# Gates, last weights and last-row operands of a Fourier-Hyena layer issued at other places, and one sum in another pool

## The chip, the cores and the metric

The kernel runs on one core of a Trainium2 chip. The metric is the device time of one execution in microseconds, the median of several. The engines are TensorE (PE in the profile; PEld is its weight load), VectorE (DVE), ScalarE (ACT), GpSimd (POOL) and SyncE (SP, which here only issues DMAs). Every engine runs its instructions in the order in which the program holds them.

## The reference

Two sequences of 1024 rows and 1024 channels go through one layer, each by itself. What is computed, cut to its steps:

```python
p = rmsnorm(x, g_pre) @ w_in
fv, fg, hv, hg, mg = jnp.split(p, [F_WIDTH, 2 * F_WIDTH, 2 * F_WIDTH + 3 * H_WIDTH,
                                   2 * F_WIDTH + 4 * H_WIDTH], axis=-1)
fz = jnp.fft.fftn(fv grouped by 256 channels, axes=(1, 3), norm="ortho").real
y_f = (fz * jax.nn.silu(fg)) @ w_fourier_out
v, x1, x2 = jnp.split(short_conv(hv, w_short), 3, axis=-1)
kf = hyena_filters(...)
z = v
for n, gate in enumerate((x1, x2)):
    z = gate * long_conv(z, kf[:, n], hyena_d[n])
y_h = (z * jax.nn.silu(hg)) @ w_hyena_out
g_f, g_h = jnp.split(jax.nn.sigmoid(mg + b_merge), 2, axis=-1)
out = (g_f * y_f + g_h * y_h) @ w_out
return x + rmsnorm(out, g_post)
```

The long convolution is one of length 2048 in the frequency domain.

## The kernel before, in words

A product of two f32 matrices is made of three matmuls. Each operand is split (`split`, L168) into a rounded part `h`, which ScalarE makes as a cast, and the rest `l`, a subtraction on VectorE or GpSimd; `hh`, `hl` and `lh` are summed (`mm3`). So every weight block of 128x512 comes as one DMA (`wr` or `mraw`), one cast (`wh`) and one subtraction (`wl`). `split` keeps the cast's instruction as `self.rounded`.

The stages, by the span's time: the Fourier branch (0 to 222 us); the Hyena filters (to 650); the branches (`branches`, to about 1700); the remaining gates of the second sequence (`phase_gates`, to 1942); the two output projections and the merge (`phase_out`, to 2302); the product with `w_out` and the last norm (`last_rows`, to the end).

`branches` runs 30 convolutions, steps (sequence b, order n, channel block c). A round of the loop issues `front` and `gates` of step i+1 and then `conv_back` of step i: its products with the filter (`k`, a DMA for each of eight groups), the spectrum `y`, its split into `yh` and `yl`, and the inverse transform `pT`. `gates` makes the multiplier `x` of a step. For b = 0 and n = 1 it also makes the SiLU gate: two halves `sg` of 128x512, loaded from memory for the early blocks (SyncE) or read from PSUM for the others, a Silu on ScalarE, and a multiply `x <- x, sg` on GpSimd. The slots of `sg` have the tag `gt`, three of them, which `gt` copies of other gates use too. GpSimd also makes the `wl` of the input projections (`pin`) here and stores `wh` and `wl` for later use.

`phase_gates` runs jobs of seven block products in place of eight (sums of blocks of both operands in advance). `kept` (L1052) copies a partial product out of PSUM: `u` into a slot of its own, `m` and `v` into the slots tagged `w` of pool `wp`, two of them, which the raw weights `wr` of `phase_out` take afterwards.

`phase_out` runs four units (a sequence and a half of it), each with 16 projections of 24 matmuls (`pyf` for Fourier, `pyh` for Hyena). Each projection takes two weights (`weight`: DMA issued by GpSimd, cast on ScalarE, subtraction on VectorE), and `gated` loads a gate `g`, opens it by a Sigmoid on ScalarE and multiplies. `ahead` splits the operands of the next pass. `beside` spreads the preparation of `w_out` over units 1 and 2: `load` in one step and `blocks` two steps later (split of blocks into `bh` and `bl`, sums, split of sums into `th` and `tl`, two stores to `d_t`). In unit 3 `sum4` loads a stored sum (`t4l`) and splits it into `t4h` and `t4l` at once.

`last_rows` runs eight jobs of seven products (`po`). `prepare` loads the merged rows (`mraw`, by GpSimd), splits blocks into `wh`, `wl` and sums of blocks (`ms`) into `mxh`, `mxl`. In a job's loop `kept` copies `u` and `v`; `prepare` of the next job is written behind the copy of `v`, and the products of T4 come last.

The order on each engine comes from a scheduler that works from the written program; `tc.issue_after(ins)` makes what is issued under it stand behind the instruction `ins` where both are on one engine. A tile that takes a slot of a pool waits until the slot's last user is done.

Of the kernel before, what the change touches and what calls it, by code (L numbers as in the profile page):

```python
# [16 lines left out]
P = 128  # L17
# [144 lines left out]
class K:  # L162
# [5 lines left out]
    def split(self, h, l, src, eng="pool", heng="act"):  # L168
        nc = self.nc
        if heng == "act":  # L170
            self.rounded = nc.scalar.copy(h, src)  # L171
        else:
            nc.vector.tensor_copy(h, src)
        self.sub(eng, l, src, h)

# [3 lines left out]
    def tt(self, eng, out, a, b, op):  # L179
        e = self.nc.gpsimd if eng == "pool" else self.nc.vector  # L180
        e.tensor_tensor(out, a, b, op=op)  # L181

# [3 lines left out]
    def sub(self, eng, out, a, b):  # L186
        self.tt(eng, out, a, b, SUB)

# [718 lines left out]
    def branches(self, nb, nct, ws):  # L907
# [10 lines left out]
        plain = list(self.PLAIN)  # L918
        Z, X = {}, {}

# [5 lines left out]
        def gates(i):  # L926
            b, n, c = steps[i]
            x = self.conv(2 + n, c, ws, f"x{n + 1}", b)
            if n and b == 0:
                early = c < NH  # L930
                ps = None if early else self.inproj(4, c)
                for q in range(2):
                    sg = self.wp.tile([P, 512], F32, tag="gt", name="sg", bufs=3)
                    if early:
                        nc.sync.dma_start(sg, self.d_g[0][4][c][:, 512 * q:512 * q + 512])
                    with tc.issue_after(self.turned.ins):
                        nc.scalar.activation(sg, sg if early else ps[:, 512 * q:512 * q + 512], AF.Silu)
                    self.mul("pool", x[:, 512 * q:512 * q + 512], x[:, 512 * q:512 * q + 512], sg)
            X[i] = x
        B = front(0)  # L940
        gates(0)
        for i, (b, n, c) in enumerate(steps):
            nxt = None
            if i + 1 < len(steps):
                nxt = front(i + 1)
                gates(i + 1)
                if i + 2 < len(steps) and steps[i + 2][0] != steps[i + 1][0]:
                    self.load_x(steps[i + 2][0])
            y = self.conv_back(n, c, B, ws)
            B = nxt  # L950
            for _ in range({4: 2, 3: 2, 2: 2, 1: 2}.get(len(steps) - i, 0)):
                self.spill_gate(b, *plain.pop(), ws)
            z = self.gate(n, c, y, X.pop(i))
            if n == 0:
                Z[c] = z
                continue
            nc.sync.dma_start(self.d_sh[b][c], z)
            if b == 0 and NF <= c:
                self.spill_gate(0, 0, c, ws)
# [22 lines left out]
    def phase_gates(self):  # L982
# [6 lines left out]
        with ExitStack() as es:  # L989
# [61 lines left out]

            def kept(p, own=False):  # L1052
                t = gw.tile([P, 512], F32, tag="u", name="u", bufs=1) if own else wp.tile([P, 512], F32, tag="w", name="m", bufs=2)
                copied = nc.scalar.copy(t, p)
                if own:
                    self.copied = copied
                return t
# [8 lines left out]
            for i, (sec, c) in enumerate(jobs):  # L1066
# [5 lines left out]
                self.times(pa, A["s1"], T1, False)  # L1072
                v = kept(pa)
                out(sec, c + 1, 1, pc, v, SUB)
# [16 lines left out]
    def phase_out(self):  # L1091
# [6 lines left out]
        with ExitStack() as es:  # L1098
# [17 lines left out]
            def weight(w, dt, q):  # L1116
# [9 lines left out]
                self.split(h.rearrange("p a b -> p (a b)"), l.rearrange("p a b -> p (a b)"), r, "dve", "act")  # L1126
                self.weighed = self.rounded
                return h, l
# [33 lines left out]
            def beside(i, dt):  # L1162

                with tc.issue_after(self.fetched.ins), tc.issue_after(self.opened.ins):
                    if i in (1, 2):
# [3 lines left out]
                        elif part == 3:  # L1169
                            blocks(k, self.raw)  # L1170
                    if (i, dt) == (3, 1):
# [14 lines left out]
            def blocks(k, r):  # L1186
# [5 lines left out]
                BL.append(l)  # L1192
                self.sums(s, r)
                h, l = [bl.tile([P, 2, 512], F32R, tag=f"{t}{k}", name=f"{t}{k}", bufs=1) for t in ("th", "tl")]
                self.split(h, l, s[:, 1:3], "dve", "act")
# [12 lines left out]
            def sum4(k):  # L1208
                h, l = [sp.tile([P, 512], F32R, tag=f"yf{2 * k + j}", name=f"t4{'hl'[j]}{k}", bufs=1) for j in range(2)]
                r = l.bitcast(F32)  # L1210
                nc.sync.dma_start(r, self.d_t[1][:, k])
                self.split(h, l, r, "dve", "act")
                T4.append((h, l))
# [31 lines left out]
    def last_rows(self, units, B11, B21, B22, T1, T2, T3, T4, gp, op):  # L1245
# [38 lines left out]
        def kept(p, own=False):  # L1284
            t = wp.tile([P, 512], F32, tag="gt" if own else "w", name="u" if own else "m", bufs=3 if own else 2)
            nc.scalar.copy(t, p)
            return t
# [10 lines left out]
        for i, (u, t) in enumerate(jobs):  # L1298
# [32 lines left out]
            self.times(pa, A["s2"], T2, False)  # L1331
            w = kept(pa, True)
            pc = self.psum("T", 2, "po")
            self.times(pc, A["s3"], T3, True)
            self.times(pa, A["s1"], T1, False)
            v = kept(pa)
            half_row(1, 1, pc, v, SUB, "pool")
            last = (A, pa, pc)
            if i + 1 < len(jobs):
                A = prepare(i + 1)  # L1340
                pa, pb, m1 = first(A)
            A_, pa_, pc_ = last

# [95 lines left out]
```

## Time and profile before

| | us |
|---|---|
| median of 3 runs (lowest to highest) | 2466.59 (2461.57 to 2469.35) |
| profiled execution | 2470.75 |
| its span, first to last instruction | 2469.0 |
| VectorE busy | 1912.8 |
| ScalarE busy | 1064.4 |
| GpSimd busy | 499.0 |
| mean granted TensorE clock | 0.994 of full |

A row of the timeline has the start, the duration, the engine, the line, the operation, what it writes and reads, and in brackets the idle time of the engine just before it with what ended that wait. The view of waits has a row for each kind of wait: its total, how often, and the longest. A row of DMA issues (SPq or POOLq, or POOL with DMA_DIRECT2D) gives the time of the issue, not of the transfer.

### The profile page before, as it was taken

How to read it: one execution, taken by the hardware profiler on the slowest of the kernel's cores; microseconds unless marked ns; L12 is line 12 of the kernel's file. 1: busy time of each engine (PE TensorE's matmuls, PEld its weight loads, DVE VectorE, ACT ScalarE, POOL GpSimd, SP SyncE). 2: the span in 40 equal slices, each digit the busy share in tenths (PEclk: the TensorE clock that was granted, in tenths of full speed). 3: DMA queues.
4: the chain of work that ended last, by engine and by line, in shares of the span. 5: the costliest groups of instructions: out<-in, count | busy, mean ns of one | idle time of the engine just before them, and what ended most of it. 6: DMA issues, size and time to landing. Idle time of an engine off the chain costs nothing.

```text
span 2469.0 us, 36969 instructions
## 1 busy us (share of the span) xinstructions
PE 2407.5 (98%) x13196; PEld 2086.9 (85%) x13196; DVE 1912.8 (77%) x3597; ACT 1064.4 (43%) x1919; POOL 499.0 (20%) x516
## 2 busy tenths in 40 slices
PE   6999999999999999999999999999999999999998
PEld 6988888888788888888888888888788788787786
DVE  7687898998649999899889999866556455665677
ACT  5546576766433333333222222323444344444343
POOL 1331213221342443331000000112100111112121
PEclk9999999999999999999999999999999999999999
DMA  7535655555555455545443443435444567775443
GB/s 274 183 122 205 217 182 166 169 180 168 171 174 179 159 176 163 172 149 203 137 134 131 143 142 131 133 128 176 161 162 158 193 218 255 237 268 194 156 160 128
DMA packets 225153, 429.37 MB, mean 174 GB/s; under 512 B 23542, under 2 KB 87255, under 8 KB 224456
## 3 DMA queue, kind: packets, MB, share of 16 engines
q1 hardware_dynamic: 198444, 333.34, 40.7%
q0 software_dynamic: 26336, 93.65, 10.7%
q8 instruction: 104, 1.70, 0.3%
q14 instruction: 81, 0.66, 0.1%
q10 hardware_dynamic: 188, 0.02, 0.0%
HBM read 290.60 MB, written 136.31 MB: 173 GB/s over the span
## 4 chain that ended last, share of the span: by engine, by line
PE 44%; DMA 4%; issue 4%; DVE 1%; POOL 1%; ACT 1%; SPq 0%; DVEq 0%; POOLq 0%; ACTq 0%
PE pin L194 17%; PE pg L194 8%; PE po L194 6%; PE pT L194 4%; PE pyf L194 4%; PE pX L194 4%; PE pyh L194 1%; DMA wr<-in_w_ho 1%; DMA wr<-in_w_fo 1%; POOL wr L1123 1%; PE tph L791 1%; DMA mraw<-d_m 1%; DMA d_m<-yf 1%; DMA t4l<-d_t 0%; DMA d_g<-gt 0%
## 5 line engine op out<-in xcount | busy, mean ns | idle before, releaser
L194 PE MATMUL pin<-xh,wl 128*128 128x512 f32 x1472 | 578.7, 393 | 3.3 <-POOL wl L181 3.3
L194 PE MATMUL pin<-xh,wh 128*128 128x512 f32 x1472 | 578.9, 393 | 1.1 <-DMA wh<-d_w 1.1
L194 PE MATMUL pin<-xl,wh 128*128 128x512 f32 x1472 | 577.5, 393 | 0.6 <-DVE xl L181 0.6
L181 POOL TENSOR_TENSOR wl<-wr,wh 128x512 fp32r<-128x512 f32 x136 | 246.2, 1811 | 1142.8 <-ACT wh L171 739.2
L194 PEld LDWEIGHTS pin<-xh,wl 128*128 128x128 f32 x1472 | 277.8, 189 | 54.9 <-POOL wl L181 4.1
L194 PEld LDWEIGHTS pin<-xl,wh 128*128 128x128 f32 x1472 | 277.7, 189 | 51.8 <-DVE xl L181 1.0
L194 PEld LDWEIGHTS pin<-xh,wh 128*128 128x128 f32 x1472 | 278.0, 189 | 51.3 <-DMA wh<-d_w 1.7
L171 ACT CAST wh<-wr 128x512 fp32r<-128x512 f32 x264 | 162.9, 620 | 326.1 <-PE pin L194 109.4
L194 PE MATMUL pT<-cinv,yh 128*128 128x256 f32 x1024 | 192.4, 283 | 4.4 <-ACT yh L171 4.4
L194 PEld LDWEIGHTS pT<-cinv,yh 128*128 128x128 f32 x1024 | 165.0, 191 | 13.9 <-ACT yh L171 4.9
L171 ACT CAST yh<-y 128x512 fp32r<-128x512 f32 x128 | 79.5, 621 | 202.5 <-DVE y L181 148.0
L181 DVE TENSOR_TENSOR t<-pX,k 128x1024 f32<-128x1024 f32 x128 | 155.5, 1215 | 14.2 <-PE pX L194 13.6
L194 PE MATMUL pyf<-sf,wh 128*128 128x512 f32 x512 | 159.1, 393 | 2.0 <-ACT wh L171 2.0
L194 PE MATMUL pX<-bh,cfwd 128*128 128x256 f32 x768 | 159.7, 286 | 0.0
L194 PE MATMUL pyh<-sh,wh 128*128 128x512 f32 x512 | 158.0, 390 | 1.6 <-ACT wh L171 1.6
L171 ACT CAST bh<-b 128x512 fp32r<-128x512 f32 x144 | 88.9, 619 | 135.1 <-DVE b L181 79.5
L181 DVE TENSOR_TENSOR wl<-wr,wh 128x512 fp32r<-128x512 f32 x128 | 87.4, 686 | 76.7 <-ACT wh L171 76.7
L194 PE MATMUL pT<-cinv,yl 128*128 128x256 f32 x512 | 145.3, 284 | 0.5 <-DVE yl L181 0.5
L194 PEld LDWEIGHTS pX<-bh,cfwd 128*128 128x128 f32 x768 | 125.8, 191 | 3.3
L194 PEld LDWEIGHTS pyf<-sf,wh 128*128 128x128 f32 x512 | 96.7, 189 | 22.8 <-ACT wh L171 2.8
L181 DVE TENSOR_TENSOR bl<-b,bh 128x512 fp32r<-128x512 f32 x144 | 102.6, 721 | 16.6 <-ACT bh L171 16.3
L194 PEld LDWEIGHTS pyh<-sh,wh 128*128 128x128 f32 x512 | 96.0, 188 | 22.2 <-ACT wh L171 2.5
(347 smaller groups left out, 5255.6 us busy)
## 6 DMA issues: line engine op xcount, KB each, us to landing
k<-d_k SPq DMA_DIRECT2D x128, 512.0 KB, 3.9
wr<-in_w_in SPq DMA_DIRECT2D x136, 256.0 KB, 3.1
d_g<-gt SPq DMA_DIRECT2D x124, 256.0 KB, 2.7
d_k<-kt SPq DMA_DIRECT2D x128, 128.0 KB, 2.2
d_k<-kt SPq DMA_DIRECT2D x64, 256.0 KB, 2.5
wr<-in_w_fo POOLq DMA_DIRECT2D x64, 256.0 KB, 3.3
g<-d_g SPq DMA_DIRECT2D x64, 256.0 KB, 3.7
wr<-in_w_ho POOLq DMA_DIRECT2D x64, 256.0 KB, 3.3
```

Of the source, the lines that this page charges most:

```text
L171: self.rounded = nc.scalar.copy(h, src)
L181: e.tensor_tensor(out, a, b, op=op)
L194: return self.nc.tensor.matmul(out, lhsT, rhs, start=start, stop=stop, skip_group_check=shared)
L791: nc.tensor.transpose(tp[:, q * P:(q + 1) * P], eo[:, e, q], self.ident)
L1123: nc.gpsimd.dma_start(r, a[w][dt][:, 512 * q:512 * q + 512])
```

## The change

- In `branches` the two halves `sg` are allocated together, and loaded in `gates` as before; the Silu of an early block and both multiplies go to a new function `close`, which is called for step i+1 behind `conv_back` of step i. The Silu stands behind `self.rounded`, the last cast of that `conv_back`. The Silu of the later blocks stays in `gates`.
- In `phase_gates` the copy `v` of the last job takes a slot of the tag `f` of pool `gw` instead of `w` of `wp`.
- In `phase_out` `blocks` is cut in two: the sums' split and the stores become `sums`, two steps later. All of `beside` also goes behind `self.weighed2`, the last `wl`.
- `sum4` only loads; the split of the T4 operands goes to the first job's round of `last_rows`, behind its copy of `v`.
- In `last_rows` `prepare` of the next job goes behind the copy of `u`.

```diff
@@ split, sub
-        self.sub(eng, l, src, h)
+        self.left = self.sub(eng, l, src, h)
...
@@ branches
-        Z, X = {}, {}
+        Z, X, G = {}, {}, {}
...
+                sg = [self.wp.tile([P, 512], F32, tag="gt", name="sg", bufs=3) for q in range(2)]
                 for q in range(2):
-                    sg = self.wp.tile([P, 512], F32, tag="gt", name="sg", bufs=3)
+                    s = slice(512 * q, 512 * q + 512)
                     if early:
-                        nc.sync.dma_start(sg, self.d_g[0][4][c][:, 512 * q:512 * q + 512])
-                    with tc.issue_after(self.turned.ins):
-                        nc.scalar.activation(sg, sg if early else ps[:, 512 * q:512 * q + 512], AF.Silu)
-                    self.mul("pool", x[:, 512 * q:512 * q + 512], x[:, 512 * q:512 * q + 512], sg)
+                        nc.sync.dma_start(sg[q], self.d_g[0][4][c][:, s])
+                    else:
+                        nc.scalar.activation(sg[q], ps[:, s], AF.Silu)
+                G[i] = sg, early
             X[i] = x
+
+        def close(i):
+
+            if i in G:
+                sg, early = G.pop(i)
+                for q in range(2):
+                    s = slice(512 * q, 512 * q + 512)
+                    if early:
+                        with tc.issue_after(self.rounded.ins):
+                            nc.scalar.activation(sg[q], sg[q], AF.Silu)
+                    self.mul("pool", X[i][:, s], X[i][:, s], sg[q])
...
             y = self.conv_back(n, c, B, ws)
+            close(i + 1)
@@ phase_gates
-            def kept(p, own=False):
-                t = gw.tile([P, 512], F32, tag="u", name="u", bufs=1) if own else wp.tile([P, 512], F32, tag="w", name="m", bufs=2)
+            def kept(p, own=False, last=False):
+                if own or last:
+                    t = gw.tile([P, 512], F32, tag="u" if own else "f", name="u" if own else "v", bufs=1 if own else 3)
+                else:
+                    t = wp.tile([P, 512], F32, tag="w", name="m", bufs=2)
...
-                v = kept(pa)
+                v = kept(pa, last=i + 1 == len(jobs))
@@ phase_out
-                self.weighed = self.rounded
+                self.weighed, self.weighed2 = self.rounded, self.left
...
-                with tc.issue_after(self.fetched.ins), tc.issue_after(self.opened.ins):
+                with tc.issue_after(self.fetched.ins), tc.issue_after(self.opened.ins), tc.issue_after(self.weighed2.ins):
...
                         elif part == 3:
-                            blocks(k, self.raw)
+                            self.sum = blocks(k, self.raw)
+                        elif part == 5:
+                            sums(k, self.sum)
...
                 self.sums(s, r)
+                return s
+
+            def sums(k, s):
                 h, l = [bl.tile([P, 2, 512], F32R, tag=f"{t}{k}", name=f"{t}{k}", bufs=1) for t in ("th", "tl")]
...
-                r = l.bitcast(F32)
-                nc.sync.dma_start(r, self.d_t[1][:, k])
-                self.split(h, l, r, "dve", "act")
+                nc.sync.dma_start(l.bitcast(F32), self.d_t[1][:, k])
@@ last_rows
-            nc.scalar.copy(t, p)
+            self.copied = nc.scalar.copy(t, p)
...
             w = kept(pa, True)
+            fetched = self.copied
...
-            last = (A, pa, pc)
+            last, kept_v = (A, pa, pc), self.copied
             if i + 1 < len(jobs):
-                A = prepare(i + 1)
+                with tc.issue_after(fetched.ins):
+                    A = prepare(i + 1)
                 pa, pb, m1 = first(A)
+            if i == 0:
+                with tc.issue_after(kept_v.ins):
+                    for h, l in T4:
+                        self.split(h, l, l.bitcast(F32), "dve", "act")
```

How the order on ScalarE changes at three places. The first is in the branches, the rows that run in the profile before between 977 and 1000 us; `L937 ACTIVATE sg` is the Silu. Before:

```order
L171 CAST wh<-wr 128x512
L171 CAST bh<-b_11100 128x512
L937 ACTIVATE sg<-sg 128x512
L171 CAST yh<-y 128x512
L171 CAST bh<-b_11101 128x512
L171 CAST wh<-wr 128x512
L758 ACTIVATE v<-pin,wsh 128x1024
```

And now:

```order
L171 CAST wh<-wr 128x512
L171 CAST bh<-b_11100 128x512
L171 CAST yh<-y 128x512
L171 CAST bh<-b_11101 128x512
L171 CAST wh<-wr 128x512
L758 ACTIVATE v<-pin,wsh 128x1024
```

No Silu is left between the `yh` casts here; the nearest pair stands 18 rows on, behind the last `yh` of a convolution, at a place that ran at about 1023 us before:

```order
L171 CAST bh<-b_11375 128x512
L838 COPY T1s<-pT 128x512
L171 CAST yh<-y 128x512
L950 ACTIVATE sg<-sg 128x512 x2
L171 CAST bh<-b_11376 128x512
L171 CAST wh<-wr 128x512
L758 ACTIVATE x_12095<-pin,wsh 128x1024
```

The second place is where `phase_out` begins, behind the eight casts of its first operands `sf` (1937 to 1957 us before); `m` and `v` are the copies of the last gate job, `g` the Sigmoids. Before:

```order
L1054 COPY m_20553<-pg_20453 128x512
L171 CAST wh_20648<-wr_20646 128x512
L171 CAST wh_20756<-wr_20754 128x512
L171 CAST sh1_20728<-sh1_20728 128x512
L171 CAST wh_20666<-wr_20664 128x512
L171 CAST wh_20710<-wr_20708 128x512
L171 CAST sh0_20682<-sh0_20682 128x512
L1153 ACT_TABLE_LOAD
L1153 ACTIVATE g_20685<-g_20685,bm_70 128x512
L1153 ACTIVATE g_20731<-g_20731,bm_70 128x512
L171 CAST wh_20738<-wr_20736 128x512
```

And now:

```order
L1070 COPY v_20553<-pg_20453 128x512
L171 CAST wh_20710<-wr_20708 128x512
L171 CAST sh0_20682<-sh0_20682 128x512
L171 CAST wh_20738<-wr_20736 128x512
L1169 ACT_TABLE_LOAD
L1169 ACTIVATE g_20685<-g_20685,bm_70 128x512
L1169 ACTIVATE g_20731<-g_20731,bm_70 128x512
L171 CAST wh_20756<-wr_20754 128x512
L171 CAST sh1_20728<-sh1_20728 128x512
```

The numbers tell the buffers apart: TensorE reads the weights in the order 20648, 20666, 20692 (cast earlier), 20710, 20738, 20756. The first two have left this stretch: `wh_20648` now stands ahead of the cast `s4h`, and `wh_20666` between the cast `a2h` and the copy `u`, all of the last gate job. `wh_20738`, which stood behind the first two Sigmoids, stands ahead of them, and `wh_20756` has gone behind them.

The third place is the first job of `last_rows` (2304 to 2325 us before); `m` and `u` are copies out of PSUM, `sq` belongs to the norm. Before:

```order
L171 CAST mxh_23722<-ms_23710 128x512
L1286 COPY m<-po 128x512
L171 CAST wh<-mraw 128x512 x3
L1316 ACTIVATE sq,ss<-o 128x512
L1286 COPY u<-po 128x512
L171 CAST t4h_23691<-t4l_23692 128x512
L171 CAST mxh_23829<-ms_23825 128x512
L171 CAST mxh_23833<-ms_23824 128x1024
L1286 COPY m<-po 128x512
L171 CAST wh<-mraw 128x512
```

And now:

```order
L171 CAST mxh_23714<-ms_23702 128x512
L1305 COPY m<-po 128x512
L1335 ACTIVATE sq,ss<-o 128x512
L1305 COPY u<-po 128x512
L171 CAST wh<-mraw 128x512 x2
L171 CAST mxh_23821<-ms_23817 128x512
L171 CAST mxh_23825<-ms_23816 128x1024
L1305 COPY m<-po 128x512
L171 CAST t4h_23418<-t4l_23419 128x512
L171 CAST t4h_23507<-t4l_23508 128x512
L171 CAST t4h_23596<-t4l_23597 128x512
L171 CAST t4h_23685<-t4l_23686 128x512
```

`u` has moved ahead of the `mraw` casts, one of those has gone to the next job, and the four `t4h` casts, three of which stood between `wh` casts in `phase_out`, stand behind the copy `m`.

More of the change, by code (lines that the diff above doesn't have):

```diff
@@ L180, in tt @@
         e = self.nc.gpsimd if eng == "pool" else self.nc.vector
-        e.tensor_tensor(out, a, b, op=op)
+        return e.tensor_tensor(out, a, b, op=op)
     def add(self, eng, out, a, b):
@@ L186, in sub @@
     def sub(self, eng, out, a, b):
-        self.tt(eng, out, a, b, SUB)
+        return self.tt(eng, out, a, b, SUB)
     def mul(self, eng, out, a, b):
```

## The prediction

> **What bounds the kernel now.** I read the busy shares of the page first, then what TensorE waits for in the whole span, then the timeline around each of its longer waits.
>
> ```profile
> PE 2407.5 (98%) x13196; PEld 2086.9 (85%) x13196; DVE 1912.8 (77%) x3597; ACT 1064.4 (43%) x1919; POOL 499.0 (20%) x516
> ```
>
> TensorE is busy for 98% of the span and the change alters neither the number nor the shape of any instruction, so all that it can win are TensorE's waits and the slow matmuls behind them. The view of its waits (in total, times, longest) has these rows at places where the change moves work:
>
> ```profile
> PE pT L194 <- ACT yh L171: 4.4, 1, 4.4
> ...
> PE po L194 <- ACT u L1286: 2.0, 1, 2.0
> PE pyf L194 <- ACT wh L171: 2.0, 2, 1.6
> PE pyh L194 <- DVE wl L181: 1.8, 2, 1.3
> PE pyh L194 <- ACT wh L171: 1.6, 2, 1.5
> ...
> PE pyf L194 <- DVE wl L181: 0.5, 1, 0.5
> ```
>
> That is 12.3 us of idle time. A wait costs more than its idle time, as the timeline of TensorE shows at the longest:
>
> ```profile
> 984.46 0.39 PE L194 MATMUL pin<-xl,wh 128*128 128x512 f32 x1
> ...
> 985.14 0.39 PE L194 MATMUL pin<-xl,wh 128*128 128x512 f32 x1
> ...
> 994.83 0.41 PE L194 MATMUL pin<-xh,wh 128*128 128x512 f32 x1
> ```
>
> From 984.46 to 985.14 three matmuls start, one every 0.227 us. From 985.14 to 994.83 there are two of half width and eleven of full width to start (the last is that at 994.83): some 2.7 us of work, and 9.69 us pass. So the wait of 4.4 us costs **7.0 us**, because the matmuls behind it start every 0.43 us until 994.8. I count the others in the same way.
>
> **A, SiLU gates one convolution later.** ScalarE, VectorE, SyncE's queue and GpSimd before the 7.0 us:
>
> ```profile
> 981.33 0.68 DVE L181 TENSOR_TENSOR y<-t 128x512 f32<-128x512 f32 x1
> ```
> ```profile
> 988.78 0.63 ACT L937 ACTIVATE sg<-sg 128x512 f32<-128x512 f32 x1 [7.13 <-DMA sg<-d_g]
> ```
> ```profile
> 986.19 0.32 SPq L935 DMA_DIRECT2D sg<-d_g x1
> ```
> ```profile
> 978.54 8.84 POOL L181 TENSOR_TENSOR x<-x,sg 128x512 f32<-128x512 f32 x2 [6.58 <-ACT wh L171]
> ```
>
> The spectrum `y` is ready at 982.0, but its rounding `yh` stands on ScalarE behind a Silu, which waits for a gate's DMA, which SyncE issues at 986.19, when the first of two GpSimd multiplies gives its slot back (7.6 us after 978.54; the second took the rest of the 8.84). The Silu is for a multiply some 45 us later (at 1032, below). In the changed order the Silu stands behind the last `yh` of its round, so this `yh` can run at 982.0 and the matmul at 985.37 as its predecessors did. I take the whole **7.0 us**; nothing else in those rows is late, since `y` comes 3 us early.
>
> What moves: six pairs of Silus (1.2 us each pair), six pairs of multiplies and most of the twelve gate loads. ScalarE is busy for 43%, and behind the moved Silus stand `bh` or `T1s`. The place to which the multiplies of 978.54 go is just ahead of this weight, and the SyncE load goes ahead of this `k`:
>
> ```profile
> 1028.08 1.30 POOL L181 TENSOR_TENSOR wl<-wr,wh 128x512 fp32r<-128x512 f32 x1 [4.18 <-ACT wh L171]
> ...
> 1032.26 2.55 POOL L181 TENSOR_TENSOR x<-x,sg 128x512 f32<-128x512 f32 x2 [1.84 <-issue]
> ```
> ```profile
> 1034.19 0.40 PE L194 MATMUL pin<-xh,wl 128*128 128x512 f32 x1
> ```
> ```profile
> 1027.06 0.32 SPq L803 DMA_DIRECT2D k<-d_k x1
> ```
> ```profile
> 1037.23 1.22 DVE L181 TENSOR_TENSOR t<-pX,k 128x1024 f32<-128x1024 f32 x1
> ```
>
> The pair can begin at about 1024, behind GpSimd's stores. At 2.55 us it ends before `wl` could begin: cost nothing. At 8.84 us, as at 978.54, it ends at 1032.8 and `wl` at 1034.1, just in time for the matmuls at 1034.19; `k` would be issued 5 us late, and its product comes 10 us after the issue. So the cover is some 5 us for `wl`, and a pair up to about 9 us is free. I take 0; the other end is the slower rival below.
>
> **B, a sum in another room.** In the last gate job `v` takes a slot of another pool, so the first weights of the projections find theirs free a job part earlier.
>
> ```profile
> 1954.24 0.39 PE L194 MATMUL pyf<-sf,wl 128*128 128x512 f32 x1
> ...
> 1960.83 0.39 PE L194 MATMUL pyf<-sf,wl 128*128 128x512 f32 x1
> ```
> ```profile
> 1932.05 0.59 ACT L1054 COPY u<-pg 128x512 f32<-128x512 f32 x1 [2.33 <-PE pg L194]
> ...
> 1954.98 0.72 ACT L1153 ACTIVATE g<-g,bm 128x512 f32<-128x512 f32 x1 [2.88 <-DMA g<-d_g]
> 1955.61 0.60 ACT L171 CAST wh<-wr 128x512 fp32r<-128x512 f32 x1
> ```
> ```profile
> 1931.15 0.54 POOL L1123 DMA_DIRECT2D wr<-in_w_fo x1 [36.02 <-DVE gt L181]
> 1941.43 1.07 POOL L1123 DMA_DIRECT2D wr<-in_w_fo x2 [9.74 <-DVE gt L181]
> ```
> ```profile
> 1934.52 0.39 PE L194 MATMUL pg<-th,s13h 128*128 128x512 f32 x1
> ```
> ```profile
> DMA to landing us min/median/max: 2.9/5.2/6.9
> ```
>
> Between 1954.24 and 1960.83 twelve matmuls start, 2.7 us of work: a loss of 3.9 us, plus some 0.7 at the shorter of the two `pyf` waits. Its `wh` waited behind a Sigmoid for that Sigmoid's DMA. Afterwards the weight of 1941.43 takes the slot that 1931.15 took, and the cast in question, `wh_20738`, stands ahead of the Sigmoids. The one that stands behind them now, `wh_20756`, is wanted twelve matmuls later, at about 1957.2, and can run at 1955.6 as the other did. But the second `wh` now stands ahead of `u`: its weight is issued at 1931.15, lands at 1934.0 with the shortest landing, and `u` ends at about 1935.2, while the matmuls of 1934.52 write into what `u` empties. I put a new wait of 1.0 us against the 4.6 (0.2 with everything early; 4.5 with the median landing and slow matmuls behind it): **3.5 us**, between 0 and 4.4.
>
> **C, last weights in three pieces.** VectorE at one of the `wl` waits (the matmul comes at 2102.47 instead of 2101.0):
>
> ```profile
> 2100.59 1.22 DVE L181 TENSOR_TENSOR tl<-osum,th 128x1024 fp32r<-128x1024 f32 x1
> 2101.73 1.28 DVE L181 TENSOR_TENSOR wl<-wr,wh 128x512 fp32r<-128x512 f32 x2
> ```
>
> Without `tl` ahead of it, `wl` ends 1.2 us earlier, and the loads and blocks also go behind a `wl`. The waits on `wl` are 2.3 us and slow matmuls behind them make it 2.9; 0.3 stays at 2102. The sums go two steps on, to where the same `tl` and a `th` cost about 1 us of the weights' lead; the lead there I can't price nearer than 0 to 1 us for the four places together. I take **2.4 us** (1.4 to 2.9).
>
> **D, operands rounded behind a copy.** The T4 operands were rounded as their loads were issued:
>
> ```profile
> 2281.03 0.62 ACT L171 CAST t4h<-t4l 128x512 fp32r<-128x512 f32 x1 [5.52 <-DMA t4l<-d_t]
> ...
> 2318.08 0.62 ACT L171 CAST t4h<-t4l 128x512 fp32r<-128x512 f32 x1 [2.50 <-DMA t4l<-d_t]
> ```
>
> ScalarE waits 5.52 us for that DMA with a `wh` behind it for which TensorE waits 1.46 us, and the same happens once more with a short wait. The rounding goes behind a copy of the second last-rows job, which comes about when the last load lands (2318), and ahead of that job's last products, which use them. Four casts and four subtractions of 0.6 to 0.7 us stand there beside an engine that waits for copies. 1.6 us of idle and 0.6 of slow matmuls: **2.2 us** (1.5 to 2.4).
>
> **E, `u` ahead of the next job's weights** in the last rows.
>
> ```profile
> 2312.83 1.66 ACT L171 CAST wh<-mraw 128x512 fp32r<-128x512 f32 x3 [6.72 <-DMA mraw<-d_m]
> ...
> 2315.02 0.56 ACT L1286 COPY u<-po 128x512 f32<-128x512 f32 x1
> ```
> ```profile
> 2313.26 0.39 PE L194 MATMUL po<-th,mxh 128*128 128x512 f32 x1
> ...
> 2319.62 0.40 PE L194 MATMUL po<-t1l,mxh 128*128 128x512 f32 x1
> ...
> 2320.54 0.40 PE L194 MATMUL po<-bh,wl 128*128 128x512 f32 x1
> ```
> ```profile
> 2314.70 2.37 DVE L181 TENSOR_TENSOR ms<-mraw 128x512 f32<-128x512 f32 x2
> ...
> 2317.59 1.41 DVE L181 TENSOR_TENSOR ms<-ms,mraw 128x512 f32<-128x512 f32 x2
> ```
>
> `u` stands behind three casts that wait for DMAs; eleven starts from 2313.26 to 2319.62 take 6.36 instead of 2.5 us, a loss of 3.9. With `u` ahead of the casts it goes. Next is late: VectorE now makes the four `ms` sums ahead of the two `wl`, and the sums wait for the `mraw` that lands about when the casts end, 2314. Four sums and one `wl` at 0.6 us end at about 2317.1; TensorE, 3.9 us earlier than before, wants it at 2316.6. I put 0.9 us against it (0 to 3, with slow matmuls): **3.0 us**.
>
> **The sum:** 7.0 + 3.5 + 2.4 + 2.2 + 3.0 = 18.1 us. The profiled run took 2470.75 us (span 2469.0 and 1.75 around it): 2452.7. It lies 4.2 us above the median of the runs, 2466.59, from which the sum gives 2448.5. I predict **2451 us**, between the two.
>
> Of the slow matmuls, which make some 8 of the 18 us: by the Trainium skill, "TensorE: Matmul & The Clock Gate", section "Why this matters for your kernels", the clock falls behind idle gaps of more than about 3 us. By that rule the gaps of B and E (1.6 and 2.0 us) would cost their idle time alone, and the sum would be some 4 us less; the rows after 1954.24 and 2313.26 show slow matmuls behind them, so the measurement decides.
>
> **The rivals.**
> *Moved multiplies hold the queues, but only here and there.* For: one multiply of the pair at 978.54 took some 7.6 us, the pair at 1032.26 2.55 us. If two of the six pairs are slow enough that `wl` is 2 to 3 us late, half of that again in slow matmuls, A is given back: 18.1 − 7 = 11, 2455 to 2460 us. Against: the 5 us of cover.
> The Trainium skill, "SBUF — State Buffer", section "Who interferes with whom", has the mechanism: a GpSimd instruction that reads SBUF and a VectorE one with two SBUF inputs block each other for a whole instruction. The trace agrees as far as 8.84 against 2.55 us goes, and by that rule the new place is no safer than the old.
> *The transitions don't gain.* In B to E only the first late thing was seen; if the second stands right behind it (a new wait for `u` or `wl` with slow matmuls), they give 3 instead of 11 us: 2457 to 2461.
> *The change does not do what it says:* the scheduler's order on record leaves that little room, but a DMA, a few us later in another run, can make another `yh` late. No gain beyond 3 us: 2464 to 2468.
> *Slower:* all six moved pairs take as long as two slow multiplies, 15.2 us. Then each next `wl` is 6 us late beyond its cover, and with half as much again in slow matmuls that costs 9 us six times: 54 − 18 = 36 us slower, about 2503. It decides from pairs of some 11 to 12 us at all six places (9 us are covered, and 18 us of gain over six places is 3 us each, slow matmuls included). Against: the longest pair in the trace is 8.84 us.
>
> **How the numbers follow.** Forecast 0.58, multiplies 0.12, transitions 0.16, nothing 0.09, slower 0.05. The low end is every stall gone with none new, 7.0 + 4.6 + 2.9 + 2.4 + 3.9 = 20.8 from the median, 2446, less 3 for what the runs differ; the high end takes in the two rivals with a part of the gain, 2461, plus 2: **2443 to 2463**. What differs by less than 0.3% (7.4 us) can hardly be told from no change. Faster by more has the forecast and most of the two partial rivals, 0.78; within it 0.17; slower 0.05.
>
> **What would show it.** A: no wait of `pT` on `yh` near 985, `yh` at about 982. Right or wrong for its price: the multiplies of the gates near 785, 845, 900, 960, 1024 and 1083, their duration and the `wl` behind each. B: no `pyf` wait near 1955, a short one of `pg` on `u` near 1934.5. C: no `pyh` or `pyf` wait on `wl`. D: `wh` casts near 2275 without 5 us of idle time ahead. E: `u` ahead of the casts that end at 2314.5, and a short wait on `wl` 2 to 3 us behind those. I am wrong if TensorE's waits behind 225 us sum to more than half of what they were, or if a wait of over 2 us stands between 750 and 1110.

## The result, and the profile after

The changed kernel takes 2453.03 us (median of 6 runs, 2447.63 to 2453.83) against 2467.52 us before (6 runs, 2461.57 to 2470.69). The ratio is 0.994, its 95% interval 0.9925 to 0.9954: 14.5 us less, with 11 to 18.5 inside the interval. The profiled execution took 2453.04 us with a span of 2451.0, so from one profile to the other 18.0 us went. The forecast was 2451, in a range of 2443 to 2463, and a sum of 18.1.

TensorE's part of the page, after:

```profile
PE 2401.8 (98%) x13196; PEld 2084.3 (85%) x13196; DVE 1915.8 (78%) x3597; ACT 1063.0 (43%) x1919; POOL 505.1 (21%) x516
```

In the view of TensorE's waits the rows that the prediction started from (`pT` on `yh`, `po` on `u`, `pyf` and `pyh` on `wh` and `wl`) are gone, but for waits of under 0.2 us; in a second profile of the changed kernel two of them are back, `pyh` on `wl` with 1.2 us and `pyf` on `wh` with 1.0. What stands there behind the Fourier stage are these, in total, times, longest:

```profile
PE pin L194 <- POOL wl L181: 2.4, 2, 2.1
...
PE pX L194 <- DVE bl L181: 1.3, 1, 1.3
...
PE pin L194 <- DMA wh<-d_w: 1.0, 1, 1.0
...
PE pg L194 <- DVE wl L181: 0.9, 1, 0.9
...
PE pT L194 <- DVE yl L181: 0.7, 1, 0.7
```

The first, third and fourth were there before too. Those on `bl` and part of that on `yl` are new. The same stretches in both kernels show where the time went. The columns are the stretch, its length, busy time and instructions of PE, PEld, DVE, ACT and POOL, the granted clock, the DMA share and GB/s. Before:

```profile
950.00:1000.00 50.00, 45.55 (x253) 39.64 (x252) 43.36 (x76) 15.49 (x25) 21.61 (x17) 0.93 0.49 160
1090.00:1115.00 25.00, 25.00 (x152) 22.24 (x150) 25.00 (x41) 7.18 (x13) 11.22 (x9) 1.00 0.37 127
...
1940.00:1965.00 25.00, 22.95 (x91) 17.56 (x90) 10.21 (x16) 9.76 (x15) 4.29 (x8) 0.93 0.71 261
...
2270.00:2300.00 30.00, 28.20 (x121) 22.09 (x120) 15.27 (x25) 10.26 (x18) 3.76 (x7) 1.00 0.61 193
2300.00:2330.00 30.00, 28.01 (x117) 22.69 (x116) 17.45 (x26) 11.33 (x22) 4.76 (x6) 0.94 0.45 140
```

After:

```profile
950.00:1000.00 50.00, 50.00 (x299) 44.41 (x298) 47.11 (x80) 18.71 (x30) 29.28 (x20) 1.00 0.54 182
1090.00:1115.00 25.00, 22.63 (x133) 19.34 (x132) 24.88 (x39) 7.35 (x14) 11.51 (x9) 1.00 0.46 148
...
1940.00:1965.00 25.00, 25.00 (x112) 20.67 (x112) 11.32 (x18) 12.46 (x20) 4.29 (x8) 1.00 0.67 230
...
2270.00:2300.00 30.00, 30.00 (x134) 24.86 (x133) 13.90 (x22) 9.79 (x17) 3.94 (x6) 1.00 0.62 197
2300.00:2330.00 30.00, 29.85 (x132) 24.38 (x131) 24.68 (x46) 14.11 (x28) 8.21 (x6) 1.00 0.39 131
```

In the four stretches that the prediction named, idle TensorE time (but for 0.15 us) and the low clocks (0.93, 0.93, 0.94) are gone. In the stretch 1090 to 1115, which it did not name, 2.4 us of idle time have come. A number that adds the slow matmuls: for each matmul, how much later it starts than the usual 0.227 us (0.120 for one of half width) behind the one before it, summed over a stage. Two executions of each kernel were profiled; the second of each belongs to the experiments below:

| stage (us of the span) | before | before, 2nd | after | after, 2nd | forecast gain |
|---|---|---|---|---|---|
| 950 to 1000 (A) | 7.1 | 7.3 | 0.2 | 0.1 | 7.0 |
| 1100 to 1150 | 0.9 | 0.9 | 3.6 | 3.5 | none named |
| 1900 to 2000 (B) | 4.7 | 5.6 | 0.1 | 0.1 | 3.5 |
| 2000 to 2250 (C) | 3.6 | 5.1 | 2.1 | 3.7 | 2.4 |
| 2250 to 2350 (D, E) | 6.7 | 5.7 | 0.3 | 0 | 5.2 |

The prediction named a sign of being wrong: TensorE's waits behind 225 us, idle time alone, sum to more than half of what they were. In the first pair of profiles they sum to 8.0 of 19.1 us, in the second to 11.2 of 20.7, which is over half. Of these 11.2, 2.3 us stand in the stage of C and 2.4 near 1105; the other 6.6 stand at places where the kernel before waits too. The other sign, a wait of over 2 us between 750 and 1110, did not come; the longest there is 1.3.

### The profile page after: what moved, and what is told of

Same layout as the page of the kernel before. It is cut to its first block, busy times and chain, and to the rows that moved or that the text cites. A ratio compares the mean times of both kernels' runs of the same rounds, so it can differ in the third digit from the quotient of the medians.

```text
span 2451.0 us, 36938 instructions
## 1 busy us (share of the span) xinstructions
PE 2401.8 (98%) x13196; PEld 2084.3 (85%) x13196; DVE 1915.8 (78%) x3597; ACT 1063.0 (43%) x1919; POOL 505.1 (21%) x516
## 4 chain that ended last, share of the span: by engine, by line
PE 46%; DMA 4%; issue 3%; DVE 1%; ACT 0%; POOL 0%; SPq 0%; DVEq 0%; ACTq 0%; POOLq 0%
PE pin L194 17%; PE pg L194 8%; PE po L194 6%; PE pT L194 5%; PE pX L194 4%; PE pyh L194 4%; PE pyf L194 3%; DMA wr<-in_w_fo 1%; DMA g<-d_g 1%; DMA wr<-in_w_ho 1%; PE tph L791 1%; DMA mraw<-d_m 0%; DVE wl L181 0%; DMA oraw<-in_w_out 0%; POOL wr L1139 0%
## 5 line engine op out<-in xcount | busy, mean ns | idle before, releaser
L181 POOL TENSOR_TENSOR wl<-wr,wh 128x512 fp32r<-128x512 f32 x136 | 258.7, 1903 | 1130.4 <-ACT wh L171 720.5
L181 DVE TENSOR_TENSOR bl<-b,bh 128x512 fp32r<-128x512 f32 x144 | 100.8, 708 | 15.0 <-ACT bh L171 14.8
```

Of the source, the lines that this page charges most:

```text
L181: return e.tensor_tensor(out, a, b, op=op)
```

## The experiments

Twelve kernels were run, each beside the kernel before on the same chip (its medians there: 2468.15, 2468.45, 2468.39 and 2469.67 us).

### Is the long wait chance, and do the parts add up?

`before_again` is the kernel before, unchanged.

> The kernel of before, profiled once more. Theory: the chain at 978 to 990 us (slow GpSimd multiply, late slot, late gate load, Silu ahead of the rounding yh) belongs to the order of the program, so the wait of pT on yh near 985 us is there again, 4 to 5 us long, and TensorE's waits behind 225 us sum to about 19 us as before. Rival: who comes first at the port of GpSimd and VectorE is a matter of some tenths of a us, so the long multiply is chance; then this execution has no wait of pT on yh or another one, and its span is nearer 2462 us. The waits of pyf, pyh and po at the stage changes (1.6, 1.3, 1.5 and 2.0 us) are there again by both.

2469.29 us in one run, and the wait is there again, with the same multiplies ahead of it:

```profile
PE pT L194 <- ACT yh L171: 4.6, 1, 4.6
```
```profile
976.58 8.85 POOL L181 TENSOR_TENSOR x<-x,sg 128x512 f32<-128x512 f32 x2 [6.58 <-ACT wh L171]
```

8.84 and 8.85 us: this is no chance from one execution to the next. The wait came in all six profiles of kernels whose branches are those of before, at 4.4 to 4.7 us. The waits at the stage changes are there too, but of other lengths (`pyf` on `wh` 3.1 us instead of 2.0 in total, in the same order).

`gates_only` is before with the hunks of the diff in `branches` alone.

> Before with the change in the branches alone (gates loaded as before, Silu and multiplies one convolution later). Theory: the wait of 4.4 us at 985 us and the slow matmuls behind it go and no wait of over 1 us comes between 750 and 1100: 5 to 7 us less than before, ratio about 0.9975. Rival (the long wait is chance in before and some new waits come in its place, as the 1.3 us on bl at 1106 us): 0 to 3 us less, ratio 0.999 to 1.0.

2464.83 us against 2468.15, ratio 0.9983 (0.9971 to 0.9996): by the ratio 4.2 us less (3.3 between the medians), 1 to 7 within the interval. In its profile no wait over 0.7 us stands between 700 and 1150 us. The theory's 5 to 7 us and most of the rival's 0 to 3 lie inside the interval, so the time alone does not tell them apart; the profile does, and for the theory. Late starts from 950 to 1000 fell as in the whole change, but a wait on `wl` near 1727, at a place that this part does not touch, made 4.1 us of them between 1700 and 1750, against 0.6 to 1.1 in the kernel before.

`all_but_gates` is the changed kernel without those hunks.

> The changed kernel with the branches as before: room, three pieces, rounding behind a copy and u first. Theory: the waits at 1948 to 1957, 2087 to 2191, 2282 to 2294 and 2315 us go or shrink as in the changed kernel, together 11 to 13 us less than before (ratio about 0.995), and the wait of pT on yh near 985 us is there as before. Rival (long wait is chance): the same 11 to 13 us, without a wait near 985 us in this profile, and a time within 3 us of the changed kernel's.

2457.85 us, ratio 0.9957 (0.9943 to 0.9972): by the ratio 10.6 us less (10.3 between the medians), beside a forecast of 11.1 for B to E. The wait near 985 us is 4.6 us, as the theory had it. By the ratios the two halves add to 14.8 us, by the medians to 13.6; the whole change brought 14.5.

### What holds the rounding `yh`?

`before_mul_dve`:

```diff
-                    self.mul("pool", x[:, 512 * q:512 * q + 512], x[:, 512 * q:512 * q + 512], sg)
+                    self.mul("dve", x[:, 512 * q:512 * q + 512], x[:, 512 * q:512 * q + 512], sg)
```

> Before with one edit: the multiplies of x by the SiLU gate run on VectorE, at the place in the program where they stood. Theory: at 978 us nothing holds the slot any longer (a multiply takes 0.7 us), SyncE's queue goes on, the Silu finds its data and the wait of pT on yh of 4.4 us is gone, although the Silu stands ahead of yh as before; 28 multiplies more on VectorE, of which TensorE sees little: 2 to 7 us less than before. Rival (the slow multiply is not the cause of the wait; the Silu's place alone is): the wait on yh stays, 3 us or more, behind a Silu that waits for its DMA.

2464.17 us, ratio 0.9987 (0.9974 to 1.0). No wait on `yh` stands near 985. The multiply took 1.28 us for two, and the Silu waited 1.51 us for its load instead of 7.13:

```profile
970.05 1.28 DVE L181 TENSOR_TENSOR x<-x,sg 128x512 f32<-128x512 f32 x2
```
```profile
973.60 0.63 ACT L937 ACTIVATE sg<-sg 128x512 f32<-128x512 f32 x1 [1.51 <-DMA sg<-d_g]
```

So without the slow multiply the chain does not form. It is not a test of the multiply alone, since the scheduler also put the Silu ahead of an earlier `yh` in this program. (It moves 16 multiplies, not the 28 that the expectation counts.) Of the 7 us, 4.5 came back between 1100 and 1150 (late starts 5.4 instead of 0.9), for the most part behind a new wait of `pX` on `bh` at 1138 us.

### The parts one by one

`room_blocks` is before with the room of `v` and the three pieces of the last weights.

> Before with two parts of the change: the room of v in the last gate job, and the last weights in three pieces behind a wl. Theory: no wait of pyf on wh between 1940 and 1965 (3.9 to 4.6 us with the slow matmuls in before), a wait of pg on u of 0 to 1 us near 1932, and the waits on wl between 2045 and 2200 shrink from about 3 us to 1.5 (four small ones, where the sums' split now stands); the waits near 985, 2282 and 2315 us are as before. Rival (the transfers at the stage change are the limit, not the slots): pyf waits 2 us or more near 1955 again, for a weight's DMA.

2456.71 us in one run. No matmul between 1940 and 1965 started late. The wait on `u` is there and small, 0.34 us with slow matmuls. Between 2000 and 2250 late starts sum to 2.8 us (before 3.6 and 5.1). The two parts account for 5 to 7 us of the 11.7 by which this one run is faster; the rest stands at waits that the edit does not touch, such as that on `u` near 2303, which lasts 1.6 us here and 2.0 and 2.4 in the two profiles of before.

`t4_only` is before with the hunk of `sum4` and the rounding in `last_rows`.

> Before with the rounding of the T4 operands moved behind the copy of v in the last rows' first round, nothing else. Theory: ScalarE no longer waits 5 to 6 us for t4l near 2281 and 2293, pyh does not wait for wh there (2.4 us with slow matmuls in before), and the wait of po on u near 2315 stays, 2 us or more. Rival (another load ahead of wh is as late): pyh waits for wh by a weight's own DMA, 1 us or more.

2464.65 us in one run. Between 2250 and 2300 nothing starts late (1.5 to 2.9 us before), as the theory had it. The wait of `po` on `u` near 2315 did not stay: it is gone too, against the expectation. In the kernel before, ScalarE waits for another `t4l` a little earlier, with a cast of job 0 behind it, and GpSimd issues the loads of job 1 only when that weight's `wl` has given its slot back:

```profile
2302.72 0.62 ACT L171 CAST t4h<-t4l 128x512 fp32r<-128x512 f32 x1 [4.32 <-DMA t4l<-d_t]
2303.25 0.62 ACT L171 CAST wh<-mraw 128x512 fp32r<-128x512 f32 x1
```
```profile
2305.57 1.58 POOL L1256 DMA_DIRECT2D mraw<-d_m x3 [17.21 <-DVE wl L181]
```

In `t4_only` nothing stands ahead of that cast, and the loads go out at 2299.35, 6 us sooner:

```profile
2299.35 0.54 POOL L1254 DMA_DIRECT2D mraw<-d_m x1 [12.94 <-DVE wl L181]
2300.18 1.21 POOL L1254 DMA_DIRECT2D mraw<-d_m x2 [0.30 <-PE pyh L194]
```

The three `mraw` casts then start at 2307.82 instead of 2312.83, 5.0 us sooner, and `u` behind them at 2310.02, while the products of the job come only 2.2 us sooner (the first on `th` at 2305.84 instead of 2308.04). So `u` is on time.

`prep_only` is before with `prepare(i + 1)` put behind the copy of `u`.

> Before with the preparation of the next last-rows job put behind the copy of u, nothing else. Theory: no wait of po on u near 2315 (3.9 us with slow matmuls), in its place one of po on wl 2 to 3 us later, 0.3 to 0.9 us; the waits near 2282 and 2294 stay. Rival (mraw lands too late whatever the order): po waits 2 us or more for wl or wh near 2317.

2470.17 us in one run, not less than before. No wait on `u`, and in its place this one:

```profile
2319.86 0.50 PE L194 MATMUL po<-bh,wl 128*128 128x512 f32 x1 [0.79 <-DVE wl L181]
```

Late starts from 2300 to 2350 sum to 1.3 us instead of 3.8 to 4.2, so the part does what it says. One run can't show 3 us of time.

### Is GpSimd's time free?

`mul_twice` is the changed kernel with this line made twice, so that `x` has the gate squared for the first sequence:

```diff
                     self.mul("pool", X[i][:, s], X[i][:, s], sg[q])
+                    self.mul("pool", X[i][:, s], X[i][:, s], sg[q])
```

> The changed kernel with each multiply of x by the SiLU gate made twice on GpSimd (so x has the gate squared). A pair then takes about 5.1 us in the quiet places, 7 to 9.5 in the busy ones. Theory by the prediction's cover (a pair up to about 9 us is free): no new wait of over 1 us at the six early gates from 750 to 1100, and a time within 3 us of the changed kernel's; at the two late gates near 1100 and 1125, where wl stands close behind, up to 3 us. Rival (GpSimd's time is on the path, or it blocks VectorE for as long as it runs): each doubled pair costs its 2.5 us or more, 15 to 20 us in all, shown as waits on yl, bl or wl.

2467.78 us, ratio to before 0.9998 (0.9988 to 1.0008): some 14 us slower than the changed kernel. The rival holds for the sum (it said 15 to 20), but not for each pair: of the six early gates three make TensorE wait for `bl` (0.6, 1.2 and 2.8 us), and so does one late gate (4.3 us), while behind early groups of four that took 6.4 and 8.4 us no wait comes for 10 us. The dearest early gate, and the shortest of them, on GpSimd, VectorE and TensorE:

```profile
840.66 5.03 POOL L181 TENSOR_TENSOR x<-x,sg 128x512 f32<-128x512 f32 x4
```
```profile
840.07 5.97 DVE L177 SCALAR_TENSOR_TENSOR b<-b,xt 128x128 f32<-128x128 f32 x2
845.97 0.28 DVE L177 SCALAR_TENSOR_TENSOR b<-bs,xt 128x128 f32<-128x128 f32 x1
```
```profile
848.96 0.39 PE L194 MATMUL pX<-bl,cfwd 128*128 128x256 f32 x1 [2.77 <-DVE bl L181]
```

Two small instructions on VectorE, which take 0.48 us together elsewhere, take 5.97, until the four multiplies are done. TensorE then waits for `bl`, which stands behind them. In the changed kernel the same two take 3.28 us beside two multiplies (2.54), and nothing is late. No wait on `wl` or `k`, the covers that the prediction counted, is among those that came.

### A version that beats both

`after_again` is the changed kernel once more, `wl_dve` gives VectorE some of GpSimd's subtractions and multiplies, `wl_mul_dve` all multiplies by the gates. The edits, with `self.weng` set to "dve" for the gates at the end of the filter stage and for the plain gates of the second sequence, and "pool" elsewhere:

```diff
-                self.split(*parts, r, "pool", "act")
+                self.split(*parts, r, self.weng, "act")
...
-                    self.mul("pool", X[i][:, s], X[i][:, s], sg[q])
+                    self.mul("pool" if early else "dve", X[i][:, s], X[i][:, s], sg[q])
```

> The changed kernel once more, timed beside the two below and as a second profile. Theory: 0.994 of before again, 14 to 15 us less; the waits on bl, T1s, t and yl at 1106 to 1111 us, which the single parts did not show, come from a late gate's multiply that starts on GpSimd just ahead of a subtraction on VectorE and holds it; they are there again if that order of starts is fixed, and gone if it is a matter of tenths of a us. No wait of pT on yh near 985 either way.

2452.36 us, ratio 0.9933 (0.9917 to 0.9949). The new waits are there again, all four, at 1105 to 1109 us (3.5 us of late starts in the stage). What makes them, in the changed kernel's first profile, VectorE, GpSimd and TensorE:

```profile
1100.46 3.76 DVE L181 TENSOR_TENSOR eo<-x 128x512 f32<-128x512 f32 x2
```
```profile
1100.52 2.55 POOL L181 TENSOR_TENSOR x<-x,sg 128x512 f32<-128x512 f32 x2
```
```profile
1106.70 0.38 PE L194 MATMUL pX<-bl,cfwd 128*128 128x256 f32 x1 [1.27 <-DVE bl L181]
```

The pair `eo` takes 1.28 us in the kernel before at this step, and 3.76 beside a late gate's multiplies. The program's order at this place is the old one; the parts alone (`gates_only`, `all_but_gates`) do not have the wait. In the kernel before the same multiplies hold an instruction further on for as long, and TensorE waits only 0.5 us, for `yl`:

```profile
1108.88 3.15 DVE L181 TENSOR_TENSOR y<-t 128x512 f32<-128x512 f32 x1
```

So it is a matter of where on VectorE the multiplies fall, which the order on each engine does not fix. Both profiles of the changed kernel have it in the same way. Why GpSimd comes to this place earlier there is open.

> The changed kernel with some GpSimd work given to VectorE: the wl of the gates at the end of the filter stage, the wl of the second sequence's plain gates near 1650 to 1740 us, and the multiplies of the two late gates. Theory (GpSimd and VectorE hold each other up, so short VectorE instructions in order are cheaper than long GpSimd ones): the waits on POOL wl near 653 (4 us with slow matmuls) and 1729 us go, and those at 1106 to 1111 too: 4 to 7 us less than the changed kernel. Rival (VectorE is so full there that what is added comes back as waits on kt, bl or xl): within 2 us of the changed kernel, or slower.

**2442.29 us** (2441.37 to 2443.25), ratio to before 0.9892 (0.9877 to 0.9908): 10 us less than the changed kernel beside it, more than the 4 to 7 expected. Two stretches of the changed kernel, and then of this one:

```profile
640.00:670.00 30.00, 27.86 (x137) 23.56 (x136) 17.24 (x49) 10.95 (x24) 10.36 (x4) 0.94 0.50 162
1090.00:1115.00 25.00, 22.63 (x133) 19.34 (x132) 24.88 (x39) 7.35 (x14) 11.51 (x9) 1.00 0.46 148
```
```profile
640.00:670.00 30.00, 30.00 (x154) 25.68 (x154) 19.29 (x49) 13.23 (x26) 0.00 (x0) 1.00 0.62 205
1090.00:1115.00 25.00, 25.00 (x161) 22.58 (x160) 24.77 (x45) 8.85 (x17) 4.49 (x6) 1.00 0.51 159
```

GpSimd has nothing to do in the first stretch now and 4.5 instead of 11.5 us in the second, and TensorE does not wait in either. These stages give 4.1 (2.5 against the second profile of the changed kernel, in which the clock did not fall there) and 2.5 us of late starts; 1150 to 1200, behind them, 1.3 to 1.8, and 1700 to 1750 about 1 to 2.

> The same with the multiplies of all gates on VectorE. Theory: the six early pairs cost TensorE nothing in the changed kernel (0.1 to 0.3 us of late starts in each 50 us), so this gains nothing more: within 2 us of the run before it, with about 7 us more of VectorE time. Rival (GpSimd's multiplies slow VectorE so much that taking them off frees it): 2 to 5 us less.

2448.79 us (2443.04 to 2450.74), ratio 0.9914 (0.9897 to 0.993): 6.5 us more than `wl_dve`, neither theory's number, though two of its six runs took 2443 and 2444 and the intervals overlap. In its profile 750 to 1100 is as quiet as before, and the difference stands elsewhere: late starts from 2000 to 2250 sum to 7.6 us against 1.8 in `wl_dve`, where the two programs do the same work. Whether the moved multiplies have a part in that is open.

### What the three pieces are worth

`wl_dve_whole` is `wl_dve` without the hunks on `beside`, `blocks` and `sums`.

> The fastest version so far (some GpSimd work given to VectorE) with the last weights prepared in two pieces and not behind a wl, as in the kernel of before. Theory: the three pieces are worth 1 to 3 us; without them TensorE waits for wl near 2045, 2076, 2091, 2136 and 2180 us, 2 to 4 us in all with slow matmuls, where the version with three pieces had 1 to 2.5: ratio to before 0.990 in place of 0.989. Rival (the waits only go from one place to another, and how long they are hangs on when each weight lands): the same time within 1 us and waits of the same sum at other places.

2445.01 us (2442.44 to 2446.41), ratio 0.9901 (0.9884 to 0.9917) against 0.9892: the intervals overlap. Its late starts from 2000 to 2250 sum to 4.9 us, with waits on `wl` at 2066.7, 2082.9 and 2128.4. This sum varies from one execution to another, so all profiles are set side by side. Seven without the pieces: 3.6, 4.1, 4.4, 4.7, 4.9, 5.0 and 6.1, the middle one 4.7. Seven with them: 1.8, 2.0, 2.1, 2.8, 3.7, 4.6 and 7.6, the middle one 2.8. So the pieces bring about 2 us in the middle, and less than the executions differ among themselves.

## Why the prediction was right, point by point

**A** was right in mechanism and in size: 7.1 us became 0.2, by the chain that it named (multiply, slot, SyncE's queue, load, Silu, `yh`). The rounding after, ready at 980.8 as `y` is:

```profile
980.08 0.68 DVE L181 TENSOR_TENSOR y<-t 128x512 f32<-128x512 f32 x1
```
```profile
980.85 0.62 ACT L171 CAST yh<-y 128x512 fp32r<-128x512 f32 x1 [0.44 <-DVE y L181]
```

Wrong was the step on what the moved multiplies cost, "a pair up to about 9 us is free". It looked for who waits for GpSimd, and not for VectorE, which GpSimd holds; a rival named this mutual blocking, but priced it by `wl` alone. At the real lengths (2.5 to 4.7 us) the six early pairs cost nothing, as forecast, but `mul_twice` shows that 5.0 us cost 2.8 us of waiting at one place and 8.4 us nothing at another, so no length alone is free. And a late gate's pair, whose Silu does not move and which the prediction did not count, costs 2.7 us at 1105.

**B** gave 4.6 instead of 3.5 us (5.5 from second profile to second profile). The wait on `u` against which 1.0 us was put was about nothing in both profiles of the changed kernel, 0.3 to 0.4 in `room_blocks` and `all_but_gates`, and 0.6 to 0.9 in `wl_mul_dve` and `mul_twice`: the second weight is issued at 1924.02, because the slot is free before that, and lands in 3.82 us, and the cast and `u` follow in time for TensorE:

```profile
1924.02 0.54 POOL L1139 DMA_DIRECT2D wr<-in_w_fo x1 [7.41 <-DVE wl L181]
```
```profile
1927.86 0.62 ACT L171 CAST wh<-wr 128x512 fp32r<-128x512 f32 x1 [3.33 <-DMA wr<-in_w_fo]
1928.39 0.58 ACT L1070 COPY u<-pg 128x512 f32<-128x512 f32 x1
```

By this row the issue waits for a `wl`, and not for the `gt` for which that of 1931.15 waited, on which the prediction built.

**C** was 2.4 in the forecast and gave 1.5 from one profile to the other, about 2 in the middle of seven. The term for the new place, "0 to 1 us for the four places together", was taken too near to 0: the sums' split has only moved, and where it stands now it is in the way again. VectorE in the second profile of the changed kernel, ahead of a wait of 1.2 us on the second `wl`:

```profile
2187.16 1.23 DVE L181 TENSOR_TENSOR tl<-osum,th 128x1024 fp32r<-128x1024 f32 x1 [4.57 <-ACT th L171]
2188.31 0.68 DVE L181 TENSOR_TENSOR g<-pyh,g 128x512 f32<-128x512 f32 x1
2188.91 0.68 DVE L181 TENSOR_TENSOR wl<-wr,wh 128x512 fp32r<-128x512 f32 x1
```

**D and E** gave 6.4 against 5.2. D's waits went entirely. E's new wait on `wl`, put at 0.9 us, was 0.3 us of late starts in one profile, none in the other, and 0.95 in `prep_only`. VectorE in the changed kernel has the order that was feared, four sums ahead of two `wl`:

```profile
2299.16 1.29 DVE L181 TENSOR_TENSOR ms<-mraw 128x512 f32<-128x512 f32 x2 [4.68 <-DMA mraw<-d_m]
2300.37 1.42 DVE L181 TENSOR_TENSOR ms<-ms,mraw 128x512 f32<-128x512 f32 x2
2301.70 1.29 DVE L181 TENSOR_TENSOR wl<-mraw,wh 128x512 fp32r<-128x512 f32 x2
```

What failed is that D and E were priced as separate terms. The late `mraw` that made `u` wait was itself an effect of the T4 rounding, so D alone gives both (`t4_only`, one profile, with nothing late from 2250 to 2350); E alone gives its own part less 0.95, and both together no more than D alone.

**The sum**: A 6.9, B 4.6, C 1.5, D and E 6.4, less 2.7 at 1105, is 16.7 of the 18.0 us between the profiles; the other 1.3 stand in stages that the change does not touch. The median moved by 14.5 (16.0 in the second comparison), since the profiled execution of before, at 2470.75, was slower than each of the six timed runs. The prediction's 2451, between 2448.5 and 2452.7, allowed for that. That the sum of 18.1 came so near to 18.0 is luck: B, D and E gave 2.3 us more than forecast, stages that the change does not touch 1.3, C 0.9 less, and 2.7 went at a place that it did not name.

## What to carry to other kernels

A load or activation that is issued well ahead of its use costs nothing until its DMA is late, and then it holds all that is queued behind it on that engine: put it behind the work that TensorE waits for, where there is slack of tens of us (here some 45). Cost a GpSimd operation by what VectorE has queued at that moment, not only by who reads its result; here a few short VectorE operations in its own order were cheaper than long ones on GpSimd, even where VectorE had no idle time (24.88 of 25 us). A preparation that is moved away from one wait stands ahead of another: look at the place it goes to as closely as at the one that it leaves.

## What the runs showed of the hardware

GpSimd and VectorE held each other for longer than one instruction. A multiply on GpSimd that takes 1.27 us alone took 7.6 us behind VectorE work without a gap, in all six profiles with that order (8.84 to 8.86 for the pair). The other way round, VectorE stood still through four GpSimd multiplies in a row (5.97 us for two instructions of 0.48). The Trainium skill, "SBUF — State Buffer", section "Who interferes with whom", says that the one that starts first holds the shared ports for the whole instruction; the runs agree, and in these two cases the engines took no turns between back-to-back instructions.

The long multiply of 978.54 ended at 986.1, 1.2 us after VectorE began this instruction, the first to read PSUM (`pX`) since the multiply had begun:

```profile
984.95 1.21 DVE L181 TENSOR_TENSOR t<-pX,k 128x1024 f32<-128x1024 f32 x1
```

So GpSimd seems to get its turn when VectorE reads PSUM. In the kernel before, between 660 and 1700 us, 34 subtractions and multiplies of this size on GpSimd took over 1.5 us. For 24 of them the last 1.27 us begin, to within 0.1 us, where VectorE begins an instruction that reads PSUM, which is one in four of its instructions there. The other ten do not fit, and no run tested it.

TensorE's granted clock fell to half for 3.4 us behind idle gaps of 1.6 to 2.4 us in the kernel before, while that of 1.3 at 1106 us in the changed kernel left it at 1.00. The length of the gap does not settle it: the wait near 653 us, for the same `wl`, lowered the clock in the changed kernel's first profile (2.1 us), and not in its second (2.2 us) or in `before_again` (3.1 us). So the slow matmuls that the prediction charged to gaps of this size are what one profile showed, and no fixed price.
